# A two-layer decoder trunk on one core: where the last norm sums stand, how weights are scaled, and who computes low parts

## The chip, the cores and the metric

The kernel runs on one core of a Trainium2 chip. Its time is the device time of one execution in microseconds (us), and the figure compared is the median of several executions. The core has a matrix engine (TensorE, PE in the profile; its weight loads are PEld), a vector engine (VectorE, DVE), an activation engine (ScalarE, ACT), GpSimd (POOL) and SyncE (SP), which issues the DMAs. Each engine works through its own list of instructions in order, and waits on semaphores for the others.

## The reference

The reference is a decoder trunk of two layers over 1024 tokens of width 1024, in float32. Cut to what matters here:

```
x   = x + w_out0( concat(conv_module(h), memory_attention(h)) )   # layer 0, h = rms_norm(x)
x   = x + relu(rms_norm(x) @ w_in0)**2 @ w_out_mlp0               # MLP, 1024 -> 4096 -> 1024
kv  = rms_norm(x) @ w_kv                                          # keys and values, made once
x   = x + w_out1( concat(nsa_attention(q, kv), memory_attention(q)) ), q = rms_norm(x) @ w_in
x   = x + relu(rms_norm(x) @ w_in1)**2 @ w_out_mlp1
```

Every rms_norm multiplies a row of x by the inverse root of its mean square and by a gain for each of the 1024 features.

## The kernel before

**Split products.** To keep float32 accuracy with a faster matmul, each operand is held as a high part (`hl[:, 0]`, rounded by ScalarE, L110) and a low part (what the rounding lost, a subtraction, L111). A product is three matmuls: high by high, high by low, low by high (L407 to L409, L448 to L450, L80 to L82). So each weight tile of 128x512 takes a DMA into a buffer `raw`, a ScalarE copy and a subtraction, the last on the engine that `k.lo_eng` names: GpSimd for the weights of the MLPs and output projections, VectorE for those of the attention (`ka`).

**Scaled weights.** The projections into keys, values and queries (`proj`, tile `ps_tok`) take weights that carry the gain of each input feature. `weight` is then called with `scales`, one column of gains for each stretch of 256 (or 292) columns of the tile. For each, ScalarE writes the rounded, scaled high part (L116) and VectorE the scaled low part (L117).

**Halves and stages.** The 1024 tokens are two halves (hf0, hf1) of 512 columns. The program runs: layer 0; the output projection `w_out` and MLP of layer 0 for hf0; `w_out` of layer 0 and the MLP for hf1, with the projections and attention of hf0 (`attend(0)`) woven between; `w_out` of layer 1 and the last MLP for hf0, with `attend(1)` woven between; then, with nothing left to weave, `w_out` of layer 1 and the last MLP for hf1, to the end. A small queue in the program (`k.pe`, `k.run`) and the framework's scheduler, which works with a model of time, lay the woven work into each engine's list. So an edit of one kind of instruction shifts the order around it on every engine.

**`w_out` and the MLP's norm.** `w_out` takes two output tiles at a time (`ps_wo`, a pair), 48 matmuls; VectorE then adds the residual (L411) and frees the two banks of PSUM, ScalarE squares the result, and `sq_add` adds the squares into `acc` (L141). While attentions are woven in, two banks serve all of `ps_wo`, `ps_i` and `ps_mo`; in the last stage there are four. After its four pairs the rows are scaled for the next matmul (`act`, L416 on ScalarE, L417 on VectorE). `inv_rms` sums `acc` over the partitions by matmuls against ones (`ps_n`, L151), takes the inverse root on VectorE (`rsqrt`, three steps on tiles of four columns, L93 to L97), spreads it by a diagonal (L157) and a matmul (L165), and copies it to `r`. The MLP applies `r` to its first products, so that matmuls `ps_i` may begin before `r` exists: in the last stage `mlp` with `both` takes two tiles of `ps_i` (48 matmuls) and asks for the two steps of `inv_rms` between.

**After the MLP** each tile of x gets its sum (`ps_mo`, L470). **After an attention** its result goes through DRAM (`mixd`, L1077) and comes back as `mix` (L387), is split into `act` (L87, L88), and the next `w_out` can start.

## Time and profile before

| | |
|---|---|
| median of 3 runs | 2445.08 us (2444.04 to 2449.28) |
| the profiled execution, its own time | 2451.38 us |
| its span in the trace | 2449.6 us |
| mean granted TensorE clock | 0.988 |
| TensorE busy | 2362.6 us, 96% of the span, 12098 matmuls |
| VectorE busy | 1669.2 us, 68% |
| ScalarE busy | 1293.3 us, 53% |
| GpSimd busy | 1229.9 us, 50% |

The first lines give the time that is compared and the execution from which all rows below come; it is one execution, 0.26% above the median. The busy times say how much of the span each engine worked. The clock is the mean of what was granted to TensorE, 1.0 being 2.4 GHz; in single stretches it is half that.

### The profile page before, as it was taken

How to read it: one execution, taken by the hardware profiler on the slowest of the kernel's cores; microseconds unless marked ns; L12 is line 12 of the kernel's file. 1: busy time of each engine (PE TensorE's matmuls, PEld its weight loads, DVE VectorE, ACT ScalarE, POOL GpSimd, SP SyncE). 2: the span in 40 equal slices, each digit the busy share in tenths (PEclk: the TensorE clock that was granted, in tenths of full speed). 3: DMA queues.
4: the chain of work that ended last, by engine and by line, in shares of the span. 5: the costliest groups of instructions: out<-in, count | busy, mean ns of one | idle time of the engine just before them, and what ended most of it. 6: DMA issues, size and time to landing. Idle time of an engine off the chain costs nothing.

```text
span 2449.6 us, 36781 instructions
## 1 busy us (share of the span) xinstructions
PE 2362.6 (96%) x12098; PEld 1994.6 (81%) x12098; DVE 1669.2 (68%) x3590; ACT 1293.3 (53%) x2938; POOL 1229.9 (50%) x1060
## 2 busy tenths in 40 slices
PE   5998899999988999999999999999999999999999
PEld 4887687888777988888887888888888887788887
DVE  7897586998668667777436866778787765333333
ACT  5575555333545457777434545666766654333332
POOL 2876544545643256566445324565566542344443
PEclk9999999999999999999999999999999999999999
DMA  5212433323344332322335443322222226233233
GB/s 186 80 55 84 151 97 101 102 92 95 123 128 141 112 115 84 91 79 79 114 103 171 136 130 92 112 64 67 80 80 63 62 67 206 69 95 97 93 96 103
DMA packets 157214, 250.87 MB, mean 102 GB/s; under 512 B 17632, under 2 KB 48992, under 8 KB 156512
## 3 DMA queue, kind: packets, MB, share of 16 engines
q1 hardware_dynamic: 157024, 248.52, 33.0%
q8 instruction: 96, 1.57, 0.3%
q14 instruction: 94, 0.77, 0.1%
HBM read 217.52 MB, written 20.45 MB: 97 GB/s over the span
## 4 chain that ended last, share of the span: by engine, by line
PE 62%; DVE 4%; DMA 3%; issue 2%; ACT 1%; POOL 1%; SPq 0%; ACTq 0%; DVEq 0%; POOLq 0%
PE ps_i L448 7%; PE ps_i L450 7%; PE ps_i L449 7%; PE ps_mo L80 6%; PE ps_mo L82 6%; PE ps_mo L81 6%; PE ps_t L1054 4%; PE ps_s L1010 4%; PE ps_o L1070 2%; PE ps_o L1073 2%; PE ps_tok L688 1%; PE ps_tok L687 1%; PE ps_tok L689 1%; PE ps_wo L409 1%; PE ps_wo L407 1%
## 5 line engine op out<-in xcount | busy, mean ns | idle before, releaser
L111 POOL TENSOR_TENSOR hl<-raw,hl 128x512 fp32r<-128x512 f32 x596 | 778.6, 1317 | 873.8 <-ACT hl L110 830.7
L110 ACT ACTIVATE hl<-raw 128x512 fp32r<-128x512 f32 x648 | 405.1, 630 | 631.6 <-PE ps_i L450 258.1
L470 DVE TENSOR_TENSOR x<-x,ps_mo 128x512 f32<-128x512 f32 x512 | 348.3, 683 | 136.8 <-PE ps_mo L82 133.4
L80 PE MATMUL ps_mo<-hid,hl 128*128 128x512 f32 x1024 | 409.3, 400 | 6.9 <-DVE x L470 6.7
L448 PE MATMUL ps_i<-act,hl 128*128 128x512 f32 x1024 | 407.5, 398 | 8.2 <-DVE x L411 6.9
L450 PE MATMUL ps_i<-act,hl 128*128 128x512 f32 x1024 | 405.7, 396 | 0.0
L449 PE MATMUL ps_i<-act,hl 128*128 128x512 f32 x1024 | 404.0, 395 | 1.2 <-DVE act L417 1.2
L82 PE MATMUL ps_mo<-hid,hl 128*128 128x512 f32 x1024 | 401.2, 392 | 0.0
L81 PE MATMUL ps_mo<-hid,hl 128*128 128x512 f32 x1024 | 400.9, 391 | 0.0
L448 PEld LDWEIGHTS ps_i<-act,hl 128*128 128x128 f32 x1024 | 193.7, 189 | 49.4 <-DVE x L411 7.3
L80 PEld LDWEIGHTS ps_mo<-hid,hl 128*128 128x128 f32 x1024 | 192.3, 188 | 49.5 <-DVE x L470 12.7
L456 DVE SCALAR_TENSOR_TENSOR a<-ps_i,r 128x512 f32<-128x512 f32 x128 | 88.0, 689 | 206.5 <-PE ps_i L450 201.6
L449 PEld LDWEIGHTS ps_i<-act,hl 128*128 128x128 f32 x1024 | 193.6, 189 | 41.8 <-DVE act L417 2.2
L450 PEld LDWEIGHTS ps_i<-act,hl 128*128 128x128 f32 x1024 | 193.5, 189 | 41.9 <-issue 0.5
L82 PEld LDWEIGHTS ps_mo<-hid,hl 128*128 128x128 f32 x1024 | 192.2, 188 | 41.1
L81 PEld LDWEIGHTS ps_mo<-hid,hl 128*128 128x128 f32 x1024 | 192.7, 188 | 37.0 <-issue 0.5
L1021 ACT ACTIVATE prob<-ps_s,small 128x512 f32<-128x512 f32 (+3 forms) x240 | 141.1, 590 | 83.0 <-DVE small L1019 52.7
L1040 POOL TENSOR_TENSOR prob<-prob,small 128x1024 f32<-128x1024 f32 (+3 forms) x120 | 180.0, 1524 | 1.3 <-DVE small L1034 0.8
L1062 DVE TENSOR_TENSOR PT<-ps_t,PT 128x512 fp32r<-128x512 f32 (+1 forms) x220 | 147.0, 671 | 48.2 <-ACT PT L1058 46.9
L1058 ACT ACTIVATE PT<-ps_t 128x512 fp32r<-128x512 f32 (+1 forms) x256 | 142.3, 566 | 60.9 <-PE ps_t L1054 55.0
L1010 PE MATMUL ps_s<-KS,Q 128*128 128x512 f32 (+5 forms) x552 | 143.1, 358 | 0.0
L88 DVE TENSOR_TENSOR hid<-a,hid 128x512 fp32r<-128x512 f32 x128 | 100.6, 787 | 59.0 <-ACT hid L87 58.3
(295 smaller groups left out, 4708.8 us busy)
## 6 DMA issues: line engine op xcount, KB each, us to landing
raw<-in_w_mlp_in_dram SPq DMA_DIRECT2D x256, 256.0 KB, 2.8
raw<-in_w_mlp_out_dram SPq DMA_DIRECT2D x256, 256.0 KB, 2.9
raw<-in_w_out_dram SPq DMA_DIRECT2D x64, 256.0 KB, 3.3
Q<-Q SPq DMA_DIRECT2D x160, 64.0 KB, 2.0
raw<-in_cmp_w_dram SPq DMA_DIRECT2D x32, 256.0 KB, 2.7
raw<-in_a_w_dram SPq DMA_DIRECT2D x24, 256.0 KB, 3.0
raw<-in_b_wq_dram SPq DMA_DIRECT2D x24, 256.0 KB, 2.7
mixd<-ev SPq DMA_DIRECT2D x80, 64.0 KB, 2.1
```

Source lines behind the costliest of these rows:

```text
L80: nc.tensor.matmul(ps, lhsT=lh, rhs=rh, start=(i == 0), stop=False)
L81: nc.tensor.matmul(ps, lhsT=lh, rhs=rl, start=False, stop=False)
L82: nc.tensor.matmul(ps, lhsT=ll, rhs=rh, start=False, stop=(i == n - 1))
L110: nc.scalar.activation(hl[:, 0, :n], raw[:, :n], AF.Copy)
L111: k.last_lo = k.lo_eng.tensor_tensor(hl[:, 1, :n], raw[:, :n], hl[:, 0, :n].bitcast(F32), op=ALU.subtract)
L448: nc.tensor.matmul(p_, lhsT=wh, rhs=h[kt][:, 0], start=kt == 0, stop=False)
L449: nc.tensor.matmul(p_, lhsT=wh, rhs=h[kt][:, 1], start=False, stop=False)
L450: nc.tensor.matmul(p_, lhsT=wl, rhs=h[kt][:, 0], start=False, stop=kt == KT - 1)
L470: nc.vector.tensor_add(x[o], x[o], ps)
L1010: nc.tensor.matmul(o_, lhsT=lhs, rhs=rhs, start=(n_ == 0), stop=(n_ == len(mms) - 1))
L1040: nc.gpsimd.tensor_tensor(t, t, sc[:, :, None].to_broadcast([P, 2, t.shape[-1]]), op=ALU.mult)
L1062: nc.vector.tensor_sub(PT[:, 1, :m], Tv[:, :m], PT[:, 0, :m].bitcast(F32))
```

## The change

In `weight` with scales, ScalarE first scales `raw` in place (a new line, 117 in the changed file), then one ScalarE copy over the whole tile makes the high part (118), and one subtraction over the whole tile the low part (120), in turn on GpSimd and VectorE. In `rsqrt` the order of the factors changes, so that with `m` and `t` in PSUM no instruction takes two operands from there; `col_stats` puts `m`, `t` and the last result into free columns of `ps_n`. `k.lo_eng` is VectorE for the `w_out` and the first part of the MLP that follow the projections of `attend(0)` and `attend(1)`, and GpSimd again from the second chunk of the MLP (`c == 1`); `sq_add` follows it. The squares behind the first MLP's second half go to VectorE as well, and three low parts in `conv_norm` move to it. Last, `w_out` of hf1 in layer 1 is no longer run to its end (by `list`) ahead of the MLP: its `inv_rms` is now asked for from within the MLP, and its pool `wb` stays open. (In the code, attention's projections are emitted ahead of `out0(1)` and of `w_out` of layer 1, and woven with them.)

Over the whole program, by the lists of instructions: 112 ScalarE instructions L116 and 112 VectorE instructions L117 go; 112 ScalarE scalings, 64 ScalarE copies and 64 low parts (32 on GpSimd, 32 on VectorE) come. 56 low parts L111 and 29 sums L141 move from GpSimd to VectorE, and 3 of L88. The matmuls are the same in number.

```diff
--- before.py
+++ after.py
@@ -46,7 +46,7 @@
         self.now = 0.0
         self.queue = []
         self.seq = 0
-        self.running = False
+        self.running = self.turn = False
 
     def pe(self, ns):
         self.now += ns
@@ -88,13 +88,14 @@
             (eng or nc.vector).tensor_tensor(lo, src, hi.bitcast(F32), op=ALU.subtract))
 
 
-def rsqrt(nc, r, m, t):
+def rsqrt(nc, r, m, t, last=None):
+
 
     nc.vector.tensor_scalar(r.bitcast(I32), m.bitcast(I32), -0.5, 1597463007.0, op0=ALU.mult, op1=ALU.add)
-    for _ in range(3):
-        nc.vector.tensor_mul(t, r, r)
-        nc.vector.scalar_tensor_tensor(t, t, -0.5, m, op0=ALU.mult, op1=ALU.mult)
-        nc.vector.scalar_tensor_tensor(r, t, 1.5, r, op0=ALU.add, op1=ALU.mult)
+    for i in range(3):
+        nc.vector.tensor_mul(t, r, m)
+        nc.vector.scalar_tensor_tensor(t, t, -0.5, r, op0=ALU.mult, op1=ALU.mult)
+        nc.vector.scalar_tensor_tensor(r if last is None or i < 2 else last, t, 1.5, r, op0=ALU.add, op1=ALU.mult)
 
 
 def weight(k, src, scales=None, pool=None, raw=None):
@@ -113,9 +114,10 @@
         w = n // len(scales)
         for i, g in enumerate(scales):
             s = slice(i * w, (i + 1) * w)
-            nc.scalar.activation(hl[:, 0, s], raw[:, s], AF.Copy, scale=g)
-            nc.vector.scalar_tensor_tensor(hl[:, 1, s], raw[:, s], g, hl[:, 0, s].bitcast(F32),
-                                           op0=ALU.mult, op1=ALU.subtract)
+            nc.scalar.activation(raw[:, s], raw[:, s], AF.Copy, scale=g)
+        nc.scalar.activation(hl[:, 0, :n], raw[:, :n], AF.Copy)
+        k.turn = not k.turn
+        (nc.gpsimd if k.turn else nc.vector).tensor_tensor(hl[:, 1, :n], raw[:, :n], hl[:, 0, :n].bitcast(F32), op=ALU.subtract)
     return hl[:, :, :n]
 
 
@@ -150,11 +152,13 @@
         for j in range(4):
             nc.tensor.matmul(ps[:, j:j + 1], lhsT=a[:, j * P:(j + 1) * P], rhs=k.ones[:, 0:1],
                              start=(i == 0 and j == 0), stop=(i == len(parts) - 1 and j == 3))
-    m, r, t = (k.tmp.tile([P, 4], F32, tag=n_, name=n_, bufs=2) for n_ in ("nm", "nr", "nt"))
+
+    r = k.tmp.tile([P, 4], F32, tag="nr", name="nr", bufs=2)
+    m, t, last = (ps[:, 4 * i:4 * i + 4] for i in range(1, 4))
     nc.vector.tensor_scalar(m, ps[:, 0:4], 1.0 / n, eps, op0=ALU.mult, op1=ALU.add)
-    rsqrt(nc, r, m, t)
+    rsqrt(nc, r, m, t, last)
     d = k.tmp.tile([P, 4, P], F32, tag="diag", name="diag", bufs=1)
-    nc.vector.tensor_mul(d, k.ident[:, None, :].to_broadcast([P, 4, P]), r[:, :, None].to_broadcast([P, 4, P]))
+    nc.vector.tensor_mul(d, k.ident[:, None, :].to_broadcast([P, 4, P]), last[:, :, None].to_broadcast([P, 4, P]))
     return d
 
 
@@ -409,7 +413,7 @@
                     nc.tensor.matmul(ps[i], lhsT=wl, rhs=mix[kt][:, 0], start=False, stop=kt == order[-1])
         for i in range(WG):
             nc.vector.tensor_add(x[o + i], ps[i], rs[i])
-            sq_add(k, acc, x[o + i], o + i == 0, nc.vector if o + i > 5 else None)
+            sq_add(k, acc, x[o + i], o + i == 0, nc.vector if o + i > 5 else k.lo_eng)
         k.pe(24 * WG * HF / 2.4)
     for o in range(KT):
         a, g = mix[order[o]], k.cols[:, (C_MLP0, C_MLP1)[l] + o:][:, 0:1]
@@ -474,6 +478,8 @@
 
     cur = proj_in(0)
     for c in range(NC):
+        if c == 1:
+            k.lo_eng = nc.gpsimd
         nxt = proj_in(c + 1) if c + 1 < NC else None
         proj_out(c, cur, c == NC - 1)
         cur = nxt
@@ -662,7 +668,7 @@
         t = k.tmp.tile([P, HF], F32, tag="a", name="t", bufs=2)
         nc.scalar.activation(t, c, AF.Tanh, bias=b)
         nc.vector.scalar_tensor_tensor(t, t, 1.0, z, op0=ALU.add, op1=ALU.mult)
-        a, b = split(nc, mix[i][:, 0], mix[i][:, 1], t, nc.gpsimd if n in LOP else None)
+        a, b = split(nc, mix[i][:, 0], mix[i][:, 1], t, nc.gpsimd if early and n in LOP else None)
         k.marks += [a, b] if n > 3 else []
 
 
@@ -1258,7 +1264,7 @@
                 if o == 0:
                     acc.append(acc_tile(k))
                 nc.sync.dma_start(xs[hf, :, o], x[hf][o])
-                sq_add(k, acc[0], x[hf][o], o == 0)
+                sq_add(k, acc[0], x[hf][o], o == 0, nc.vector)
             return after
 
         ka = K()
@@ -1300,6 +1306,8 @@
                       Vd)
 
         attend(0, acc)
+
+        k.lo_eng = nc.vector
         r = out0(1)
         acc = []
         mlp(k, 0, x[1], act[1], r, after0(1, acc), MIXORD)
@@ -1309,14 +1317,15 @@
         act = [act_tiles(hf) for hf in range(2)]
         x = [x_tiles(hf) for hf in range(2)]
         load_mix(k, act[0], mixd[0], MIXORD, k.wpool, "raw", k.nraw)
+        k.lo_eng = nc.vector
         rs = [w_out(k, 1, act[0], x[0], xs[0], MIXORD)]
         ka.rpool = pool(es, "rb", "right")
 
         ps3 = es.enter_context(psum_pool("ps3"))
-        with tc.tile_pool(name="wb", bufs=1, side="right") as wb:
-            ka.psum, ka.wpool, ka.tmp, ka.tag = ps3, wb, wb, "mm"
-            load_mix(ka, act[1], mixd[1], MIXORD, ka.wpool, "mix", 8)
-            rs.append(iter(list(w_out(ka, 1, act[1], x[1], xs[1], MIXORD))))
+        wb = pool(es, "wb", "right")
+        ka.psum, ka.wpool, ka.tmp, ka.tag = ps3, wb, wb, "mm"
+        load_mix(ka, act[1], mixd[1], MIXORD, ka.wpool, "mix", 8)
+        rs.append(w_out(ka, 1, act[1], x[1], xs[1], MIXORD))
         for hf in range(2):
             if hf == 1:
                 k.psum, k.nps = ps3, 4
```

Lines of the changed file stand 1 to 9 further down than before (L111 is L112, L117 became 117 to 120, L141 is L143, L151 is L153, L411 is L415, L417 is L421, L448 is L452, L470 is L474).

**VectorE at the start of the projections of `attend(0)`**, around the first sums of `ps_wo` for hf1 in layer 0. Before:

```order
L470 TENSOR_TENSOR x_2551<-x_2551,ps_mo 128x512 x2
L664 SCALAR_TENSOR_TENSOR t<-t,z 128x512
L470 TENSOR_TENSOR x_2552<-x_2552,ps_mo 128x512 x2
L88 TENSOR_TENSOR act_347<-t,act_347 128x512
L664 SCALAR_TENSOR_TENSOR t<-t,z 128x512
L117 SCALAR_TENSOR_TENSOR hl<-raw,cols,hl 128x256 x8
L411 TENSOR_TENSOR x_5968<-ps_wo,rs 128x512 x2
```

and in the changed kernel:

```order
L88 TENSOR_TENSOR act_345<-t,act_345 128x512
L143 TENSOR_TENSOR acc<-acc,sq 128x512
L88 TENSOR_TENSOR act_346<-t,act_346 128x512
L143 TENSOR_TENSOR acc<-acc,sq 128x512 x2
L120 TENSOR_TENSOR hl<-raw,hl 128x512
L112 TENSOR_TENSOR hl<-raw,hl 128x512 x2
L120 TENSOR_TENSOR hl<-raw,hl 128x512
L415 TENSOR_TENSOR x_5960<-ps_wo,rs 128x512
L158 TENSOR_SCALAR ps_n<-ps_n 128x4
L112 TENSOR_TENSOR hl<-raw,hl 128x512
L94 TENSOR_SCALAR nr<-ps_n 128x4
L415 TENSOR_TENSOR x_5960<-ps_wo,rs 128x512
```

Eight scaled low parts L117 in a row stood ahead of the two L411; now two L120, two low parts of other weights (L112) and, above them, sums of squares that were GpSimd's (L143) stand there, and the second L415 comes four instructions behind the first.

**TensorE where the `w_out` of the last stage ends and the last MLP begins** (`ps_n` are the norm sums, `ps_i` the MLP's first products). Before:

```order
L408 MATMUL ps_wo<-act_18493,hl 128x512
L409 MATMUL ps_wo<-act_18493,hl 128x512
L151 MATMUL ps_n<-ones,acc 128x1 x4
L448 MATMUL ps_i<-act_18494,hl 128x512
L449 MATMUL ps_i<-act_18494,hl 128x512
```

and in the changed kernel, 32 matmuls after the last `ps_wo`:

```order
L454 MATMUL ps_i<-act_18490,hl 128x512
L452 MATMUL ps_i<-act_18491,hl 128x512
L453 MATMUL ps_i<-act_18491,hl 128x512
L153 MATMUL ps_n<-ones,acc 128x1 x4
L454 MATMUL ps_i<-act_18491,hl 128x512
L452 MATMUL ps_i<-act_18491,hl 128x512
```

The sums stood directly behind the last `ps_wo`; now 32 of the 48 matmuls of the first two tiles of `ps_i` stand between.

**VectorE at the end of `attend(1)`**, where `mix` comes back (`ev` is the last piece of the attention, `x` the sums of the MLP that is woven in). Before:

```order
L1076 TENSOR_TENSOR ev<-ps_o,ev 64x256
L470 TENSOR_TENSOR x_18501<-x_18501,ps_mo 128x512
L470 TENSOR_TENSOR x_18498<-x_18498,ps_mo 128x512 x2
L88 TENSOR_TENSOR act_18494<-mix,act_18494 128x512
L470 TENSOR_TENSOR x_18499<-x_18499,ps_mo 128x512
L88 TENSOR_TENSOR act_18495<-mix,act_18495 128x512
L88 TENSOR_TENSOR act_18496<-mix,act_18496 128x512
L470 TENSOR_TENSOR x_18499<-x_18499,ps_mo 128x512
```

and in the changed kernel:

```order
L1082 TENSOR_TENSOR ev<-ps_o,ev 64x256
L474 TENSOR_TENSOR x_18500<-x_18500,ps_mo 128x512
L474 TENSOR_TENSOR x_18501<-x_18501,ps_mo 128x512 x2
L88 TENSOR_TENSOR act_18494<-mix,act_18494 128x512
L88 TENSOR_TENSOR act_18495<-mix,act_18495 128x512
L88 TENSOR_TENSOR act_18496<-mix,act_18496 128x512
```

Sums of the MLP stood between the splits of `mix`; now the last sums all come before them. On TensorE the last matmul of `attend(1)` (`ps_o`, from `Vc`) was followed by 54 matmuls `ps_mo` before the first `ps_wo`; in the changed kernel 18 follow it.

## Rows read from the trace of the kernel before

**Rows 1.** The page's first part: busy us, share of the span, instructions.

```profile
PE 2362.6 (96%) x12098; PEld 1994.6 (81%) x12098; DVE 1669.2 (68%) x3590; ACT 1293.3 (53%) x2938; POOL 1229.9 (50%) x1060
```

**Rows 2.** Windows: stretch, its length, each engine's busy us (count), granted clock, DMA.

```profile
650.00:800.00 150.00, 132.76 (x675) 110.97 (x674) 119.44 (x237) 81.64 (x162) 64.16 (x47) 0.95 0.47 143
...
1290.00:1500.00 210.00, 198.29 (x1156) 170.44 (x1155) 146.71 (x324) 102.09 (x208) 80.46 (x63) 0.99 0.45 137
...
2000.00:2110.00 110.00, 102.95 (x466) 83.10 (x465) 55.64 (x90) 45.84 (x77) 26.71 (x21) 0.97 0.42 137
```

**Rows 3.** Windows of 7 us behind four waits of TensorE.

```profile
691.00:698.00 7.00, 6.06 (x16) 4.80 (x17) 1.48 (x3) 2.07 (x4) 2.52 (x3) 0.56 0.66 214
777.00:784.00 7.00, 6.26 (x18) 5.00 (x19) 6.04 (x27) 3.01 (x5) 0.31 (x1) 0.61 0.13 44
2041.00:2048.00 7.00, 7.00 (x32) 5.63 (x31) 2.38 (x4) 1.98 (x4) 2.85 (x3) 1.00 1.02 377
2090.00:2097.00 7.00, 7.00 (x22) 5.85 (x23) 2.97 (x13) 0.00 (x0) 0.00 (x0) 0.53 0.00 0
```

**Rows 4.** Timeline at 685 to 692: start, us, engine, line, instruction, [idle before, releaser].

```profile
684.74 0.40 PE L409 MATMUL ps_wo<-act,hl 128*128 128x512 f32 x1
691.94 0.79 PE L407 MATMUL ps_wo<-act,hl 128*128 128x512 f32 x1 [6.80 <-DVE x L411]
...
681.06 10.23 DVE L117 SCALAR_TENSOR_TENSOR hl<-raw,cols,hl 128x256 fp32r<-128x256 f32 x8 [3.86 <-ACT hl L116]
```

**Rows 5.** Timeline at 745 to 778, of TensorE, VectorE and GpSimd.

```profile
770.45 0.40 PE L409 MATMUL ps_wo<-act,hl 128*128 128x512 f32 x1
777.74 0.80 PE L448 MATMUL ps_i<-act,hl 128*128 128x512 f32 x1 [6.90 <-DVE x L411]
...
745.30 0.68 DVE L411 TENSOR_TENSOR x<-ps_wo,rs 128x512 f32<-128x512 f32 x1
...
772.10 1.26 DVE L93 TENSOR_SCALAR hr<-hm 128x8 int32<-128x8 int32 x1
...
777.02 0.67 DVE L411 TENSOR_TENSOR x<-ps_wo,rs 128x512 f32<-128x512 f32 x1
...
773.62 3.33 POOL L111 TENSOR_TENSOR hl<-raw,hl 128x512 fp32r<-128x512 f32 x2 [0.28 <-ACT hl L110]
```

**Rows 6.** Waits of TensorE, 1290 to 1500: waited for, us in total, times, longest.

```profile
PE ps_c L820 <- DVE hT L797: 1.4, 1, 1.4
```

**Rows 7.** Timeline at 2086 to 2090, of TensorE and VectorE.

```profile
2086.62 0.40 PE L409 MATMUL ps_wo<-act,hl 128*128 128x512 f32 x1
2089.89 1.87 PE L151 MATMUL ps_n<-ones,acc 128*128 128x1 f32 x8 [2.87 <-DVE acc L141]
...
2089.15 0.68 DVE L141 TENSOR_TENSOR acc<-acc,sq 128x512 f32<-128x512 f32 x1
```

**Rows 8.** Timeline at 2024 to 2042, of TensorE, VectorE and SyncE's queue.

```profile
2024.03 0.28 PE L1070 MATMUL ps_o<-PT,Vc 128*128 128x256 f32 x1
...
2041.34 0.39 PE L407 MATMUL ps_wo<-act,hl 128*128 128x512 f32 x1
...
2040.30 0.67 DVE L470 TENSOR_TENSOR x<-x,ps_mo 128x512 f32<-128x512 f32 x1
...
2027.35 3.65 SPq L387 DMA_DIRECT2D mix<-mixd  x8
...
2033.72 1.69 SPq L107 DMA_DIRECT2D raw<-in_w_out_dram  x3
```

**Rows 9.** Lines by form: count, duration min/median/max in ns, first and last start.

```profile
L117 DVE SCALAR_TENSOR_TENSOR hl<-raw,cols,hl x112: 465/484/1541, 681.1 to 1472.0; 128x256 fp32r<-128x256 f32 x96, 128x292 fp32r<-128x292 f32 x16
L116 ACT ACTIVATE hl<-raw,cols x112: 491/500/542, 680.5 to 1471.5; 128x256 fp32r<-128x256 f32 x96, 128x292 fp32r<-128x292 f32 x16
L111 POOL TENSOR_TENSOR hl<-raw,hl x596: 1267/1296/1987, 42.4 to 2435.1; 128x512 fp32r<-128x512 f32 x199
L111 DVE TENSOR_TENSOR hl<-raw,hl x52: 674/689/1810, 36.4 to 2077.1; 128x512 fp32r<-128x512 f32 x52
```

## Prediction

> **What bounds the kernel now.** I read the page's first part before anything else: TensorE is busy for 96% of the span, VectorE for 68%, the others less [rows 1]. As the change neither adds nor removes matmuls, it can only win what TensorE spends idle or at half clock, and lose by making more of it. Next I cut the span into windows and looked for stretches where TensorE's busy time falls short. From 650 us on there are three: 17.2 us idle of 150 where the attention of the first half begins, 11.7 of 210 where that of the second begins, 7.1 of 110 around the end of that attention and the start of the last MLP [rows 2]. That is 36 us of the 87 that TensorE idles in the whole span [rows 1]; the other 51 lie at the start, in layer 0 and at the very end, where the change moves little. In these windows the granted clock is also below 1. Windows of 7 us behind the long waits show 0.56, 0.61 and 0.53 [rows 3], which is the lower level, 1.2 GHz, for most of each. Such a window costs 7 us times what is missing from 1: 3.1, 2.7 and 3.3 us.
>
> Last I read the timeline at each wait, for what comes last there.
>
> - Wait A, at 685 us: TensorE issues the last matmul of a pair at 684.74 and starts the next at 691.94, released by VectorE's L411, which frees the banks [rows 4]. A matmul at full clock is followed by the next after 0.23 us (some 31 in 7 us [rows 3]), so 7.0 us are lost. L411 was ready, but eight L117 stood ahead of it and took 10.23 us, 1.28 us each, where the median of an L117 is 0.484 us [rows 4, 9].
> - Wait B, at 770 us: 7.1 us, again for L411 [rows 5]. Here steps on tiny tiles, such as L93 on 128x8, take 1.26 us while GpSimd runs low parts of 1.3 to 1.9 us; L411 starts only at 777.02.
> - Wait C, 1290 to 1500 us: the 11.7 us are many small waits, the largest 1.4 us [rows 6].
> - Wait D, at 2087 us: the norm sums `ps_n` wait 2.87 us for the last sum L141, which ends at 2089.83; then comes the stretch at 0.53 [rows 3, 7].
> - Place E, at 2024 to 2041 us: from the last matmul of the attention to the first `ps_wo` 17.3 us pass, in which 54 matmuls `ps_mo` keep TensorE going; 54 by 0.23 is 12.4 us, so it idles for 4.9 [rows 8].
>
> **The change, part by part.** VectorE loses 112 L117, by the median 54 us [rows 9]. It gains 56 low parts, 29 sums and three splits of GpSimd's, and 32 scaled low parts, some narrower, so about 120 steps: at 0.69 us or less [rows 9] some 79 us. Net that is up to +25 us of VectorE, half of it near each attention, less what its steps no longer lose to a busy GpSimd. GpSimd loses 88 steps of 1.3 us, takes 32 back, and so gets some 70 us. ScalarE gains 64 steps, about 40 us, and at 53% [rows 1] has room for them.
>
> *A.* In the new order four subtractions of about 0.69 us, 2.8 us, stand where eight L117 took 10.2. But the second scaled low part belongs to a later weight: its buffer must come free first (there are three), through a GpSimd step of 1.3 us and a transfer. If all of that falls into the wait, 5 us remain; if none, nothing. I take 2.5 us, halfway, and since the 2.9 us of wait D were enough to be followed by the low clock, I leave that loss in place. Saved: 7.0 - 2.5 = 4.5 us, with ends 0 and 10.1.
>
> *B.* From the last L411 of the third pair (745.30) to the first of the fourth (777.02) VectorE went 31 us [rows 5], over eight L117, six L417 and steps stretched by GpSimd. The new list has two scaled low parts in place of the eight, as many L417, and four low parts and two sums more; at unstretched durations I count about 24 us (an estimate). TensorE ran for 24.5 us from 745.98 to its stop at 770.7 (770.45 [rows 5]). The wait should nearly go, and the low clock with it: of 7.1 + 2.7 = 9.8 us I take 9, with ends 3 and 10.
>
> *C.* VectorE is busy for 147 of 210 us there [rows 2]; its net gain of up to 12 us fits in, but small waits of this sort follow the order, which is new everywhere. I take +2, with ends -5 and +6.
>
> *D.* In the new order 32 matmuls, 7.3 us, stand between the last `ps_wo` and the sums, while the last L141 ends 3.0 us behind that `ps_wo` [rows 7]. So the wait is gone. The inverse root starts later but is covered by 34 more matmuls, 7.8 us. Saved: 2.9 + 3.3 = 6.2 us; if the clock falls for another reason, 2.9.
>
> *E.* Now only 18 matmuls `ps_mo`, 4.1 us, follow the attention's last one; the other 36 have moved ahead of it, where TensorE was full already. What the 17.3 us consist of does not change: result to DRAM and back (`mix` is issued at 2027.35), splits, the weights of `w_out` (issued at 2033.72, into buffers that the splits free) [rows 8]. The sums L470 that stood between the splits and ahead of the first low part (one at 2040.30) are out of the way; for these I take 1.5 us off. So 17.3 - 1.5 - 4.1 = 11.7 us idle in place of 4.9, 6.8 more. Before, the broken wait left the clock at 1.00 [rows 3]; behind one whole wait of that length I expect the lower level as behind A, B and D, 3.3 us. Together -10 us, with ends -4 and -12.
>
> *The rest.* `rsqrt` on PSUM columns has as many steps as before, off TensorE's path in the last stage; they cost nothing as long as those 34 matmuls cover them, else some tenths of a microsecond each time. The path of a scaled weight grows by a ScalarE copy and, every second time, by GpSimd's 1.3 us. TensorE takes 24 matmuls of half of 0.23 us, 2.8 us, for each; ScalarE needs 1.6 and GpSimd 0.65 on average, so the rate holds and only first weights come later. I take -2 us, with ends 0 and -15 (below).
>
> Sum: 4.5 + 9 + 2 + 6.2 - 10 - 2 = 9.7 us. The profiled execution took 2451.4 us, its span 2449.6, so 2441.7 by the sum; it lies 6.3 us above the median of the runs, and from the median 2445.1 the sum gives 2435.
>
> **A rule on the port.** L117 takes 0.484 us in the median and 1.28 where GpSimd works without a pause [rows 4, 9], and a step of 8 columns takes 1.26 beside GpSimd [rows 5]: a VectorE step with two inputs in SBUF can last until GpSimd's instruction ends. The Trainium skill, "SBUF — State Buffer", section "SBUF: two separate sides", says the same: the two engines share a port pair that is locked for a whole instruction, and a VectorE operation with two SBUF inputs is fully blocked by a GpSimd one that reads SBUF. The trace agrees, with 1541 ns as the longest L117. The rule speaks for moving steps off GpSimd, and against the 32 new low parts that it gets amid the projections, where L117 ran at 0.484.
>
> **Rivals.**
>
> *VectorE becomes the late engine (slower).* Each of the 32 GpSimd low parts may hold up a VectorE step by up to 1.3 - 0.48 = 0.8 us, 26 us in all, on top of the net 25. Around 650 to 800 us VectorE was busy for 119 of 150 us [rows 2]; with its half of the two it would need 145, and TensorE would wait for it at each L411 and each scaled weight. Then A and B save nothing, C goes to -5, the rest to -15 and D and E stay: -5 + 6.2 - 10 - 15 = -24, 2469 us; with half of that 2457. It decides from the point where A, B and C together save less than the 5.8 us by which E and the rest exceed D. Against it: GpSimd loses far more steps than it gets, the 1.28 us of A came from its unbroken work, and the short steps gain too.
>
> *The banks are freed no earlier (same).* If A's L411 still stands behind the transfer of a scaled weight and B keeps 4 us and its clock, A and B together save 3: 3 + 2 + 6.2 - 10 - 2 = -1, 2446 us. For it: the release of L411 depends on the list around it, and not on L117 alone.
>
> *E is cheaper (faster still).* If the clock stays up at E and the return of `mix` is as quick as its transfers allow, E is -4 and B 10: about 2428; with all of A 2422.
>
> That the change does not do what it says is excluded for D by the new order; for E the order shows the 18 matmuls.
>
> **How the numbers follow.** The forecast as summed, 5 to 15 us faster, gets 0.48; the faster rival 0.16; same 0.18; slower 0.18. A change within 0.2%, 4.9 us, can't be told from none here. The faster side thus has 0.64. The range leaves out one in ten at each end: 2420, where all of the faster rival comes in, to 2453, short of the half-priced slower rival.
>
> **What would show it.** Behind `ps_wo` in the last stage no wait for L141, and a clock of 1.0 at the first `ps_i`. At the end of the second attention one wait of TensorE of about 12 us for the first weights of `w_out`, and a low clock behind it. At the first L411 of the projections a wait of about 2.5 us, at the last hardly one. VectorE's busy total between 1670 and 1700, GpSimd's about 1160. I am wrong if waits for scaled low parts or for L411 in the projections add up to over 10 us in either attention, or if other work fills place E.

## The result, and the profile after

The changed kernel takes 2463.64 us, the median of six runs (2461.86 to 2465.38), and the kernel before 2448.53 us; the ratio is 1.0063, with a 95% interval of 1.0049 to 1.0076. The forecast was 10 us faster; it is 15 us slower, and outside the range. None of the rivals describes it: places D and E went as written, place B did not, and the largest part came from something that no step of the prediction had looked at.

The page of the changed kernel's profiled execution (span 2461.6 us, clock 0.984), its first part:

```profile
PE 2372.0 (96%) x12098; PEld 1994.3 (81%) x12098; DVE 1649.2 (67%) x3598; ACT 1326.1 (54%) x3002; POOL 1143.4 (46%) x1004
```

TensorE has the same 12098 matmuls as in [rows 1], but is busy for 9.4 us more. More waiting can't do that: either its clock was lower or its matmuls themselves became longer. That is the first thing to explain, and stretches at full clock tell the two apart (below). VectorE is busy for 20 us less and GpSimd for 86 us less, where the prediction had up to 30 us more for VectorE. Fewer steps stretched beside GpSimd would do that (v48 below shows it for L117), but the 20 us were not taken apart.

The same windows as in [rows 2], and two narrower ones around waits A and B (stretch, its length, busy us of TensorE, weight loads, VectorE, ScalarE, GpSimd, granted clock, DMA):

```profile
650.00:800.00 150.00, 136.43 (x693) 114.51 (x692) 115.16 (x257) 91.11 (x183) 21.72 (x19) 0.94 0.46 144
670.00:700.00 30.00, 27.17 (x116) 21.68 (x115) 23.58 (x47) 22.31 (x43) 2.66 (x2) 0.94 0.65 210
755.00:795.00 40.00, 29.26 (x162) 24.76 (x162) 34.04 (x97) 20.83 (x46) 6.21 (x5) 0.83 0.34 110
1290.00:1500.00 210.00, 200.24 (x1161) 172.44 (x1160) 141.55 (x324) 115.09 (x231) 39.45 (x36) 0.98 0.42 130
1500.00:2000.00 500.00, 497.82 (x2821) 430.97 (x2820) 384.19 (x1030) 340.01 (x936) 296.83 (x264) 1.00 0.26 79
2000.00:2110.00 110.00, 96.76 (x457) 79.86 (x456) 55.93 (x85) 44.34 (x75) 22.17 (x19) 0.94 0.39 127
```

and in the kernel before the two narrow ones, and the one from 1500 us on:

```profile
670.00:700.00 30.00, 21.73 (x84) 17.05 (x83) 17.83 (x17) 14.81 (x29) 24.53 (x18) 0.89 0.56 180
755.00:795.00 40.00, 31.45 (x175) 25.82 (x174) 35.05 (x95) 19.84 (x44) 10.76 (x9) 0.91 0.37 112
1500.00:2000.00 500.00, 500.00 (x2850) 435.04 (x2849) 386.15 (x1028) 338.50 (x938) 299.57 (x266) 1.00 0.26 76
```

Around A (670 to 700) TensorE's idle time falls from 8.3 to 2.8 us and the clock rises from 0.89 to 0.94: about 7 us won. Around B (755 to 795) idle time rises from 8.6 to 10.7 us and the clock falls from 0.91 to 0.83: about 5 us lost. Around C idle time falls from 11.7 to 9.8, which 0.01 of clock over 210 us gives back, and 2.2 us are new behind it. The last window has 13.2 us idle in place of 7.1.

What waits there, in the timeline of the changed kernel (TensorE, GpSimd and VectorE, 678 to 787 us):

```profile
678.58 0.77 PE L411 MATMUL ps_wo<-act,hl 128*128 128x512 f32 x1 [2.83 <-DVE x L474]
...
754.68 1.69 POOL L724 TENSOR_TENSOR mq<-mq,qg 128x512 f32<-128x512 f32 x1 [6.39 <-DVE mq L723]
...
755.12 1.80 DVE L421 SCALAR_TENSOR_TENSOR act<-x,cols,act 128x512 fp32r<-128x512 f32 x1
...
773.52 0.68 DVE L415 TENSOR_TENSOR x<-ps_wo,rs 128x512 f32<-128x512 f32 x1
...
774.25 0.80 PE L452 MATMUL ps_i<-act,hl 128*128 128x512 f32 x1 [4.75 <-DVE x L415]
...
782.17 0.69 DVE L112 TENSOR_TENSOR hl<-raw,hl 128x512 fp32r<-128x512 f32 x1 [1.70 <-ACT hl L111]
...
782.77 0.15 DVE L97 SCALAR_TENSOR_TENSOR ht<-ht,hr 64x1 f32<-64x1 f32 x1
...
785.96 0.22 DVE L88 TENSOR_TENSOR khl<-kcn,khl 64x64 fp32r<-64x64 f32 x1
...
786.23 0.37 PE L833 MATMUL ps_dc<-ident,khl 64*128 64x64 f32 x1 [3.98 <-DVE khl L88]
```

At A one wait of 2.83 us is left. At B L415 comes at 773.52 and TensorE has waited 4.75 us for it; in [rows 5] it was 6.90. But VectorE now waits 1.70 us for a ScalarE copy, and behind the low part L112 that needs it stand the remaining small steps of an inverse root of the attention (`ht`, L97), laid in turn with those of another root and of the norm. The tile `khl`, which comes out of that root, is made only at 785.96, and TensorE waits another 3.98 us for it. The L421 of 1.80 us runs beside GpSimd's L724: a stretched step, as in [rows 5].

The timeline from behind the second attention to the last norm sums (TensorE, ScalarE, SyncE's queue):

```profile
2041.27 0.39 PE L82 MATMUL ps_mo<-hid,hl 128*128 128x512 f32 x1
2054.90 0.79 PE L411 MATMUL ps_wo<-act,hl 128*128 128x512 f32 x1 [13.24 <-ACT hl L111]
...
2054.22 1.92 ACT L111 ACTIVATE hl<-raw 128x512 fp32r<-128x512 f32 x3 [1.40 <-DMA raw<-in_w_out_dram]
...
2047.90 2.61 SPq L108 DMA_DIRECT2D raw<-in_w_out_dram  x3
...
2109.87 0.95 PE L153 MATMUL ps_n<-ones,acc 128*128 128x1 f32 x8
```

and three windows (columns as above):

```profile
784.00:791.00 7.00, 4.77 (x19) 4.15 (x20) 5.78 (x21) 3.01 (x8) 1.46 (x2) 0.51 0.17 61
...
2055.00:2061.00 6.00, 6.00 (x15) 4.66 (x16) 1.86 (x3) 1.73 (x3) 0.00 (x0) 0.53 0.70 252
2109.00:2116.00 7.00, 7.00 (x36) 5.82 (x35) 2.52 (x12) 1.26 (x2) 3.03 (x3) 1.00 0.26 77
```

After its last `ps_mo` TensorE waits 13.24 us for the weights of `w_out`, whose transfers are issued at 2047.90, and its clock is at 0.53 for the 6 us behind. That is place E, answering to [rows 8]. The norm sums at 2109.87 have no wait, and the 7 us from 2109 on run at 1.00 where [rows 3] had 0.53: place D.

Now the longer matmuls. Two stretches of 48 each from the dense last stage, first and last start of `ps_i` and of `ps_mo`, in the changed kernel:

```profile
2203.78 0.39 PE L452 MATMUL ps_i<-act,hl 128*128 128x512 f32 x1
...
2214.75 0.39 PE L454 MATMUL ps_i<-act,hl 128*128 128x512 f32 x1
2214.98 0.39 PE L80 MATMUL ps_mo<-hid,hl 128*128 128x512 f32 x1
...
2225.65 0.39 PE L82 MATMUL ps_mo<-hid,hl 128*128 128x512 f32 x1
```

and in the kernel before:

```profile
2215.47 0.40 PE L448 MATMUL ps_i<-act,hl 128*128 128x512 f32 x1
...
2226.25 0.39 PE L450 MATMUL ps_i<-act,hl 128*128 128x512 f32 x1
2226.47 0.40 PE L80 MATMUL ps_mo<-hid,hl 128*128 128x512 f32 x1
...
2237.18 0.39 PE L82 MATMUL ps_mo<-hid,hl 128*128 128x512 f32 x1
```

From the first start to the last are 47 steps. `ps_mo` takes 10.67 us in the changed kernel, 10.71 before: 227 and 228 ns a matmul. `ps_i` takes 10.97 against 10.78 us: 233.4 and 229.4 ns, at a granted clock of 1.00 and with no wait in either. `ps_i` streams `act`, `ps_mo` streams `hid`. The list of tiles of the two built programs says where these stand in SBUF (the byte in each partition, and its remainder by 512):

```
tile          before          after
hl (weights)   4928  320       4928  320
hid           31552  320      31552  320
act, first    62592  128      62464    0
```

The change took two tiles, `nm` and `nt`, twice 32 bytes each, out of the pool `tmp`. `act` stands behind that pool, and so moved by 128 bytes, as did the tiles behind `act`, those of x among them.

### The profile page after: what moved, and what is told of

Its sections match the earlier page's. It is cut to its first block, busy times and chain, and to the rows that moved or that the text cites. A ratio compares the mean times of both kernels' runs of the same rounds, so it can differ in the third digit from the quotient of the medians.

```text
span 2461.6 us, 36812 instructions
## 1 busy us (share of the span) xinstructions
PE 2372.0 (96%) x12098; PEld 1994.3 (81%) x12098; DVE 1649.2 (67%) x3598; ACT 1326.1 (54%) x3002; POOL 1143.4 (46%) x1004
## 4 chain that ended last, share of the span: by engine, by line
PE 85%; DVE 6%; DMA 3%; issue 3%; ACT 2%; POOL 1%; SPq 0%; POOLq 0%; ACTq 0%; DVEq 0%
PE ps_i L452 9%; PE ps_i L453 9%; PE ps_i L454 9%; PE ps_mo L80 9%; PE ps_mo L82 8%; PE ps_mo L81 8%; PE ps_t L1060 4%; PE ps_s L1016 4%; PE ps_o L1076 2%; PE ps_wo L411 2%; PE ps_o L1079 2%; PE ps_wo L412 2%; PE ps_wo L413 2%; PE ps_a L80 2%; PE ps_a L82 2%
## 5 line engine op out<-in xcount | busy, mean ns | idle before, releaser
L112 POOL TENSOR_TENSOR hl<-raw,hl 128x512 fp32r<-128x512 f32 x540 | 696.2, 1300 | 759.0 <-ACT hl L111 736.4
L111 ACT ACTIVATE hl<-raw 128x512 fp32r<-128x512 f32 x648 | 405.4, 630 | 630.1 <-PE ps_i L454 251.6
L474 DVE TENSOR_TENSOR x<-x,ps_mo 128x512 f32<-128x512 f32 x512 | 348.8, 684 | 139.1 <-PE ps_mo L82 136.2
L452 PE MATMUL ps_i<-act,hl 128*128 128x512 f32 x1024 | 408.6, 399 | 7.4 <-DVE x L415 7.2
L452 PEld LDWEIGHTS ps_i<-act,hl 128*128 128x128 f32 x1024 | 192.8, 188 | 51.9 <-DVE x L415 7.4
L120 POOL TENSOR_TENSOR hl<-raw,hl 128x512 fp32r<-128x512 f32 (+1 forms) x32 | 38.5, 1205 | 219.2 <-ACT hl L118 185.5
```

The lines of the kernel that those rows point to most:

```text
L111: nc.scalar.activation(hl[:, 0, :n], raw[:, :n], AF.Copy)
L112: k.last_lo = k.lo_eng.tensor_tensor(hl[:, 1, :n], raw[:, :n], hl[:, 0, :n].bitcast(F32), op=ALU.subtract)
L452: nc.tensor.matmul(p_, lhsT=wh, rhs=h[kt][:, 0], start=kt == 0, stop=False)
L474: nc.vector.tensor_add(x[o], x[o], ps)
```

## The experiments

Theory 1 is that the time of a matmul depends on the place of the operand that it streams against the place of its weights. Theory 2 is that `ps_i` became slower by the new order of instructions or by chance of the execution. Theories D and E are the prediction's steps of that name. Each run has its own comparison with the kernel before; its median was 2447.2 to 2447.8 us in these runs.

| run | median us | ratio to before (95%) | matmuls, 2150 to 2400 us |
|---|---|---|---|
| before | 2447 | 1 | 1096 |
| the change | 2463.6 | 1.0063 (1.0049 to 1.0076) | 1088 |
| a128 | 2451.45 | 1.0018 (1.0008 to 1.0027) | 1096 |
| a320 | 2445.16 | 0.9990 (0.9981 to 1.0000) | 1104 |
| b384 | 2460.92 | 1.0056 (1.0040 to 1.0072) | 1088 |
| b192 | 2442.43 | 0.9978 (0.9968 to 0.9989) | 1104 |
| hid192 | 2454.29 | 1.0029 (1.0012 to 1.0045) | 1088 |
| all192 | 2449.16 | 1.0013 (1.0002 to 1.0023) | 1095 |
| mq320 | 2430.26 | 0.9938 (0.9920 to 0.9955) | |
| z192 | 2437.25 | 0.9960 (0.9949 to 0.9972) | |
| w48 | 2437.39 | 0.9952 (0.9937 to 0.9968) | |
| v48 | 2432.44 | 0.9933 (0.9916 to 0.9949) | |
| r80 | 2442.01 | 0.9973 (0.9964 to 0.9982) | |
| best | 2432.39 | 0.9935 (0.9920 to 0.9950) | |
| wz48 | 2429.56 | 0.9938 (0.9917 to 0.9959) | |
| wzl48 | 2431.27 | 0.9942 (0.9922 to 0.9962) | |
| wv48 | 2445.54 | 0.9993 (0.9982 to 1.0003) | |

The last column counts matmuls in a window of 250 us in the last stage, in which TensorE is busy throughout.

### The place of act

**a128, a320 (the changed kernel), b384, b192 (the kernel before).** A pool with one unused tile stands ahead of `act`; nothing else changes.

```diff
         k.rpool = k.tmp
+        pool(es, "gap").tile([P, 32], F32, name="gap")
         ap = pool(es, "act")
```

with 32 columns (128 bytes), 80, 96 and 48. The order on each engine is that of the kernel it was made from.

> The changed kernel with 128 bytes of unused room ahead of the pool of act, so that act stands at the byte it had before the change; every engine's order is that of the changed kernel. Theory 1 (the place of act in SBUF sets TensorE's pace: 229.7 ns per 512-column ps_i matmul before, 233.3 after, on some 4500 matmuls that read act): pace back to about 229.7 ns and a time of 2446 to 2450 us. Theory 2 (the pace comes from the new order of instructions, or from the execution): pace stays at 233.3 ns, time 2463.6 us.

> The changed kernel with 320 bytes ahead of the pool of act, which then stands at the same remainder by 512 bytes (320) as the weights hl and as hid, whose matmuls took 227 ns in both kernels. Theory 1: ps_i falls to about 227 ns, and the time to 2433 to 2438 us. Theory 1b (only the place of act itself counts, not against that of the weights): somewhere between 227 and 233 ns. Theory 2: 233.3 ns, 2463.6 us.

> The kernel before with 384 bytes ahead of the pool of act, so that act stands at remainder 0 by 512 as in the changed kernel, and nothing else changed. Theory 1: ps_i at 233.3 ns, some 14 to 18 us slower than before, 2462 to 2466 us. Theory 2: 229.7 ns, 2448.5 us.

> The kernel before with 192 bytes ahead of the pool of act, so that act stands at remainder 320 by 512, as hl and hid do. Theory 1: ps_i at 227 ns, 10 to 12 us faster than before, 2436 to 2439 us. Theory 2: no change, 2448.5 us.

By the pace of the matmuls theory 1 holds in all four, theory 2 in none. The times lie 1.1 us (b384) to 7.2 us (a320) outside what was expected, each on the side of a smaller effect. With `act` at remainder 0 the kernel before becomes 13.5 us slower, and the changed kernel with `act` at its old byte 12.2 us faster. At 320, where the weights and `hid` stand, both are faster than at 128. In a320 a `ps_i` takes as long as a `ps_mo` (timeline, first and last of 48):

```profile
2211.26 0.39 PE L452 MATMUL ps_i<-act,hl 128*128 128x512 f32 x1
...
2221.91 0.39 PE L454 MATMUL ps_i<-act,hl 128*128 128x512 f32 x1
```

10.65 us by 47 is 226.6 ns. The gains at 320 (5.0 us in b192, 6.3 in a320 against a128) are smaller than the 10 to 12 expected. `ps_i` alone, 2.8 ns by 3072, would give 8.6 us. The traces show what is missing: the 2.8 ns belong to the last stage. Taken over the whole program, from the start of one `ps_i` to the start of the next (full clock, steps under 260 ns), the mean is 229.5 ns before and 227.9 in b192; 1.6 ns by 3072 are 4.9 us. From 1500 to 2000 us, beside the attention, it is 230.3 and 230.4 ns, so the better place wins nothing there, while the change's place still costs: 233.5.

**hid192, all192.** The same gap in the kernel before, between the weights and `hid`, and ahead of the weights:

```diff
         k.wpool = pool(es, "w")
+        pool(es, "gap").tile([P, 48], F32, name="gap")
         k.hid = pool(es, "hid")
```

> The kernel before with 192 bytes between the pool of the weights and that of hid, so that hid stands at remainder 0 by 512, act at 320 and the weights hl at 320 as ever. Theory 1 (place of the streamed operand against the weights, for every tile alike): ps_mo from 227 to about 233 ns, ps_i at 227 ns, time about 15 us above that with act at 320, 2457 to 2462 us. Rival (something in act's pool alone): ps_mo stays at 227 ns, 2442 us.

> The kernel before with 192 bytes ahead of the weights, so that hl and hid stand at remainder 0 by 512 and act at 320: every distance between them as before, every place moved. Theory 1b (only the distance of streamed operand and weights counts): ps_mo 227 ns, ps_i 229.7 ns, time as before, 2445 to 2450 us. Rival 1a (the place of the streamed operand counts, 0 slow and 320 fast): ps_mo about 233 ns, ps_i 227 ns, 2457 to 2462 us.

The time of hid192 is 2.7 us under what was expected, that of all192 within it. In hid192 the two change roles (timeline, first and last start of 48 `ps_mo`, then of 48 `ps_i`):

```profile
2206.05 0.39 PE L80 MATMUL ps_mo<-hid,hl 128*128 128x512 f32 x1
...
2217.02 0.39 PE L82 MATMUL ps_mo<-hid,hl 128*128 128x512 f32 x1
2217.25 0.39 PE L448 MATMUL ps_i<-act,hl 128*128 128x512 f32 x1
...
2227.92 0.39 PE L450 MATMUL ps_i<-act,hl 128*128 128x512 f32 x1
```

`ps_mo` takes 10.97 us by 47, 233.4 ns, and `ps_i` 10.67, 227.0. So it is not a property of `act`. In all192 the weights, `hid` and `act` have all moved, but not against each other, and the count of matmuls (1095) is that of before; the time is 2 us above, at the edge of its interval. So the distance counts, not the place. With streamed operand and weights at the same remainder a matmul of 512 columns takes 227 ns; at a distance of 320 (streamed less weights) 229.4; at 192, which is the change's, 233.4. Within a block the weights stand at four columns of a tile, 512 bytes apart. In the changed kernel and in a320 the times of `ps_i` do not differ between these by 0.1 ns (in the kernel before the first column's are 1.4 ns longer), so I read the distance by 512.

The traces hold more distances. The `w_out` of the last stage takes its weights from another pool, `wb`, whose tiles `hl` stand at remainder 288 in the kernel before, 416 in the changed one and 320 in best (below). Its 192 matmuls `ps_wo` of 512 columns, from start to start as above:

| run | act | weights in wb | distance by 512 | ns |
|---|---|---|---|---|
| best | 320 | 320 | 0 | 226.8 |
| b192 | 320 | 288 | 32 | 233.3 |
| the change | 0 | 416 | 96 | 233.3 |
| a128 | 128 | 416 | 224 | 233.3 |
| before | 128 | 288 | 352 | 233.3 |
| a320, mq320 | 320 | 416 | 416 | 234.2, 234.3 |

So 32 bytes of distance already cost as much as any other, and 320 with its 229.4 ns is the exception.

### The end of the second attention, and the last norm sums

**mq320.** The changed kernel at 320, with the first MLP's squares left on GpSimd; by the order, 54 matmuls then follow the second attention's last one.

```diff
-                sq_add(k, acc[0], x[hf][o], o == 0, nc.vector)
+                sq_add(k, acc[0], x[hf][o], o == 0)
```

> The changed kernel except that the squares behind the first MLP stay on GpSimd, and with act at remainder 320 by 512 bytes, as in the run with 320 bytes. By the order, 54 matmuls again follow the last one of the second attention, not 18. Theory E (the missing 36 matmuls cost 8 to 9 us of waiting and 3 to 7 us of low clock): 10 to 15 us under the run with 320 bytes (2445.2), so 2430 to 2435 us. Rival (they only moved the wait, and the loss turns up elsewhere): 2443 to 2447 us.

Against a320 14.9 us are won. TensorE's waits from 2000 to 2110 us (waited for, us in total, times, longest):

```profile
PE ps_mo L80 <- DVE x L474: 2.1, 2, 1.4
PE ps_wo L411 <- ACT hl L111: 0.4, 1, 0.4
```

The wait, 13.1 us in a320, is gone, as theory E had it. But not all of the 14.9 us is E: from 1290 to 1500 us the clock is 1.00 in mq320 and 0.98 in a320, which is 4 us, and from 650 to 800 us mq320 idles 2 us more at a clock lower by 0.01. wzl48 below also shows that the price of the place alone is smaller than this pair says.

**z192.** The kernel before at 320, with the last part of the change alone (the difference for `rs.append` and `wb`, as shown in the change).

> The kernel before with the last part of the change alone (the last norm sums taken from within the MLP, pool wb left open), and act at remainder 320 by 512. Against the kernel before with act at 320 (2442.4): theory D (the 2.9 us wait and the stretch at the low clock both go): 2436 us, and no stretch at the low clock behind 2080 us. Rival (the clock falls at the change of stage anyway): 2439 to 2440 us.

5.2 us against b192, by theory D 6.4; the intervals of the two just touch. The window in which the sums stand (2088.01 us) runs at the full clock, and no wait is left in it:

```profile
2083.00:2090.00 7.00, 7.00 (x36) 5.94 (x35) 2.23 (x9) 1.68 (x3) 2.52 (x2) 1.00 0.11 38
```

### Scaling, VectorE's steps, and both

**w48, v48, r80.** The kernel before at 320 with one part each: the scaling of weights; VectorE's low parts and sums (`k.lo_eng`, and `conv_norm`); `rsqrt`. The edits are those parts of the change, with a gap that puts `act` at 320.

> The kernel before with the scaling of weights alone changed (ScalarE in place, one low part in turn on GpSimd and VectorE), act at remainder 320; compare with 2442.4 us. Theory (the run of eight L117 was what kept L411 waiting at 685 and 770 us): both waits of 7 us fall under 3 us, 2430 to 2436 us. Rival (the low parts that GpSimd gets amid the projections hold VectorE up, or the longer path of a weight does): at least one of the waits stays above 4 us, 2440 us or more.

> The kernel before with the move of low parts, of the squares in w_out and of three low parts in conv_norm from GpSimd to VectorE alone, act at remainder 320; compare with 2442.4 us. Theory (VectorE's steps are no longer stretched beside GpSimd, so the waits for L411 shrink although it has more to do): 2434 to 2439 us, the L117 at 681 to 691 us near 0.5 us each. Rival (VectorE becomes the late engine): 2444 us or more.

> The kernel before with the new order of factors in rsqrt and its columns in PSUM alone; act at remainder 320 by 512 bytes, with the gap made larger by what the removed tiles took. Theory 1 and the step of the prediction (no cost by itself, all of its effect on the time came through the place of act): 2440 to 2445 us. Rival (steps on PSUM are dearer and lie on the path): over 2447 us.

Against 2442.4 us, w48 wins 5.0, v48 10.0 and r80 nothing. r80 shows that the steps of `rsqrt` on PSUM cost nothing that these runs can see, and that what this part did to the time it did through the tiles that it removed. In w48 the waits for L411 (its line 412) are down to 0.8 us; the longest wait of TensorE from 650 to 800 us is a new one, for GpSimd's scaled low part (its line 119 is the 120 of the change):

```profile
PE ps_tok L689 <- POOL hl L119: 2.7, 1, 2.7
```

Its time is 1.4 us above what I expected. In v48 six L117 take 3.27 us in one go, where [rows 4] had eight in 10.23:

```profile
680.02 3.27 DVE L117 SCALAR_TENSOR_TENSOR hl<-raw,cols,hl 128x256 fp32r<-128x256 f32 x6 [0.23 <-ACT hl L116]
```

So they had been stretched by GpSimd, and with its steps moved away they are not. The gain is more than I had expected (2434 to 2439), and its trace does not show where all of it comes from. The two waits for L411, 6.7 and 6.9 us in b192, shrink to one of 3.2, but two others are new (TensorE, 650 to 800 us):

```profile
PE ps_n L165 <- DVE diag L157: 4.6, 1, 4.6
PE ps_wo L407 <- ACT sq L140: 4.3, 1, 4.3
PE ps_i L448 <- DVE x L411: 3.2, 1, 3.2
```

Idle time there falls from 17.4 us to 12.3, and the clock from 0.95 to 0.93, which takes 3 us of that back.

**best.** mq320 with two more gaps, on the right side of SBUF, that bring the weights of the projections and of the last `w_out` to remainder 320.

```diff
+            tc.tile_pool(name=f"gw{hf}", bufs=1, side="right") as gw, \
             tc.tile_pool(name=f"wa{hf}", bufs=1, side="right") as k.wpool:
+        gw.tile([P, 40], F32, name="gap2")
...
+        pool(es, "gap3", "right").tile([P, 24], F32, name="gap3")
         wb = pool(es, "wb", "right")
```

> As the run without the moved squares (2430.3 us, act at 320), and besides the weights of the attentions and of the last stage's w_out moved to remainder 320 too, by gaps of 160 and 96 bytes. Theory 1: the 192 matmuls of the last w_out fall from 234 to 227 ns, 1.3 us, and if the 256-column matmuls of the projections follow the same rule, 2 to 4 us more: 2425 to 2429 us. Rival (narrow matmuls don't): 2429 us.

No gain: 2432.4 against 2430.3, with intervals that overlap. The traces show both parts. The last `w_out` did as expected, 226.8 ns in place of 234.3, 1.4 us for its 192 matmuls. The projections' matmuls of 256 columns (`ps_tok`) did not follow: they take 119.7 ns from start to start at the same remainder and 118.3 in mq320. So here the rule is seen at 512 columns alone.

**wz48, wzl48, wv48.** The kernel before at 320 with scaling and norm sums; with these and VectorE's steps in the second half; with scaling and VectorE's steps in both halves (the line below ahead of `out0(1)` too, and `conv_norm`).

```diff
+        k.lo_eng = nc.vector
         rs = [w_out(k, 1, act[0], x[0], xs[0], MIXORD)]
```

> The kernel before with the scaling of weights and the last norm sums changed, nothing moved to VectorE, act at remainder 320. Theory (these two are independent and the extra steps of VectorE are what brings waits back at 760 to 780 us): 2437.4 - 5 = 2431 to 2433 us, with no wait over 3.5 us between 650 and 800 us. Rival (waits come with any new order): 2436 us or more.

> As the run before (scaling and norm sums), with VectorE's low parts and sums in the second half alone added; by the order, 18 matmuls instead of 54 then follow the second attention's last one. Theory E: 10 to 15 us above the run before, with one wait of 12 to 14 us near 2030 us and a long stretch at the low clock behind it. Rival (what that end costs is won back between 1290 and 1500 us): within 4 us of it.

> The kernel before with the scaling of weights and all of VectorE's extra steps but the squares behind the first MLP, act at remainder 320. By the order it too has 18 matmuls at the end of the second attention. Theory (the combination makes VectorE late again): between 650 and 800 us two waits of over 3 us and two stretches at the low clock, where scaling alone had none over 3; with the dear end of the attention, 2446 to 2452 us. Rival (the two parts add up): no wait over 3 us between 650 and 800 us, 2436 to 2442 us.

wv48 loses what w48 and v48 had won: 2445.5 us, 0.5 us under the range of the theory. One part of it is place E. By the order wv48 has 18 matmuls behind the second attention's last one, where w48 and v48 have 54 (v48 has the same VectorE steps: the number follows the whole order, not one part). In its trace the first `ps_wo` behind them waits 13.5 us. From 2000 to 2110 us its TensorE idles 16.3 us at a clock of 0.92, that of w48 and v48 6.3 and 7.0 us at 0.98. The other part is the first attention. The window from 650 to 800 us in w48, v48 and wv48:

```profile
650.00:800.00 150.00, 141.49 (x747) 120.11 (x746) 111.92 (x222) 97.56 (x197) 85.10 (x61) 0.99 0.47 148
...
650.00:800.00 150.00, 137.72 (x720) 117.25 (x719) 121.37 (x277) 83.75 (x168) 19.42 (x14) 0.93 0.46 146
...
650.00:800.00 150.00, 135.60 (x710) 115.01 (x710) 118.20 (x252) 91.94 (x189) 30.69 (x24) 0.94 0.45 144
```

With scaling alone TensorE idles 8.5 us there at a clock of 0.99; with VectorE's steps alone 12.3 at 0.93; with both, 14.4 us at 0.94. And the waits of TensorE in wv48, same stretch:

```profile
PE ps_n L166 <- DVE diag L158: 4.5, 1, 4.5
PE ps_wo L408 <- ACT sq L141: 4.4, 1, 4.4
PE ps_i L449 <- DVE x L412: 4.1, 1, 4.1
```

These are the three waits of v48; mq320 has them too (4.4, 4.4, 4.1). So VectorE's steps bring them, with scaling or without, and what scaling wins at the first attention is lost with them. In the changed kernel the order differs again: of its three waits (2.8, 4.7 and 4.0 us) only that for L415 is of the same kind. That such waits come from where the steps stand in VectorE's list was read from the timeline of the changed kernel above, and not tried by itself.

wz48 has the lowest median of all, with none of the other low parts and sums moved to VectorE; mq320, 0.7 us above, cannot be told from it. It is 1.4 us under its expected range, and its longest wait from 650 to 800 us is 2.8 us. Two of its windows:

```profile
1290.00:1500.00 210.00, 197.85 (x1162) 172.07 (x1161) 133.67 (x286) 114.42 (x240) 100.10 (x79) 0.98 0.40 128
2000.00:2110.00 110.00, 107.55 (x480) 86.11 (x479) 56.97 (x92) 45.53 (x75) 33.14 (x25) 1.00 0.41 141
```

and those of wzl48:

```profile
1290.00:1500.00 210.00, 199.69 (x1174) 174.28 (x1173) 141.32 (x322) 114.67 (x241) 52.34 (x46) 0.98 0.40 128
2000.00:2110.00 110.00, 96.61 (x431) 78.82 (x430) 53.70 (x90) 43.85 (x73) 18.77 (x15) 0.94 0.39 133
```

From 1290 to 1500 us wzl48 has 1.8 us less idle time, and in the last window 10.9 us more at a clock of 0.94. By the medians it is only 1.7 us slower, by the spans of the two profiles 7.5 (2434.0 and 2426.5), with runs of each from 2428 to 2437. So the expectation of 10 to 15 us failed, and its rival holds in part: some of what that end costs is won ahead of it. How much of E is net stays open between 2 and 8 us.

## Why the prediction was wrong, point by point

- **What bounds the kernel** was right for waits, and wrong in one sentence: that without more matmuls the change "can only win what TensorE spends idle or at half clock, and lose by making more of it". The time of a matmul itself can change. The changed kernel lost 12.2 us so (a128 against the change).
- **The rest** (-2) was the step that failed most. It took `rsqrt` and its PSUM columns for free, and so they are as steps (r80), but the tiles that went with them moved `act` by 128 bytes. Over the whole program the 3072 matmuls `ps_i` took 233.3 ns in place of 229.6 in a128, 11.5 us, and the 768 `ps_wo`, which stream `act` as well, 233.3 in place of 230.4, 2.2 us; by the medians the place cost 12.2 us.
- **A** (+4.5) was about +7, by the windows; the wait left was 2.8 us. That this is near the estimated 2.5 is luck: it is a wait for another step, a sum L474, and at the L415 that the estimate was about no wait is left.
- **B** (+9) failed: it was about -5. The count of VectorE's work assumed unstretched steps one behind the other with nothing awaited. The wait for L415 did shrink, to 4.75 us, but VectorE then waited for ScalarE with the small steps of inverse roots behind it, TensorE idled 4 us more, and the clock fell twice. Scaling alone (w48) does remove this wait; v48 and wv48 show that VectorE's extra steps bring waits of 3 to 5 us with them.
- **C** (+2) was nothing, with 2.2 us of new idle time behind it, from 1500 to 2000 us.
- **D** (+6.2) was right: no wait and full clock in the changed kernel, 5.2 us in z192.
- **E** (-10) was right in place and kind: 13.2 us of waiting in place of 4.9, forecast 11.7, and the low clock behind it, 6 us at 0.53, 2.8 us. Its net price is smaller (wzl48).
- **The sum** of these waits and clocks is 7 - 5 + 0 - 2 + 6 - 11 = -5 us, where +9.7 was forecast. a128, with the old place, is 4.1 us slower than before, which agrees. With the 12.2 us of the place, that makes the 16 us between the change and 2447.4.
- **The rival of a late VectorE** has its mechanism in part (v48, wv48), but not its price, and not by the route described: VectorE's busy time fell. The rule that it leaned on held up: in the Trainium skill's page "SBUF — State Buffer", section "SBUF: two separate sides", a VectorE step with two SBUF inputs is blocked by a GpSimd step that reads SBUF and began first. The trace agrees (L421 takes 1.80 us, begun 0.44 us into GpSimd's L724 of 1.69 us), and as L117's in v48 show, it worked for the move of steps off GpSimd. One row that the prediction put under this rule does not belong there: L93, 1.26 us in [rows 5], has one input. The trace of the kernel before shows that it too ended with a step of GpSimd (L111, 771.48 to 773.34; L93 to 773.36).

## What to carry to other kernels

Before pricing an edit, compare the places of the tiles that the busiest engine reads in the two built programs: an edit that removes 128 bytes can cost more than all that it saves in waits. Where TensorE is the bound and streams 512 columns against weights, put the streamed tile and the weights at the same remainder by 512 bytes; here that was worth 5 us in the kernel before, and 18 in the changed one. Two parts of a change that help alone (5 and 10 us here) can come to nothing together, because each new order of the lists can open a wait somewhere else; so each is tried alone and in pairs, and the whole timeline is read, not only the place that the edit meant.

## What the runs showed of the hardware

A matmul of 512 columns with float32r operands took 227, 229.4 or 233.4 ns at full granted clock, by the distance of its streamed operand from its weights in SBUF (0, 320 or 192 bytes by 512), with no other change, and 233.3 to 234.3 at each of the other five distances that the traces hold. Beside the attention, from 1500 to 2000 us, distance 0 lost its advantage over 320 (230.4 and 230.3 ns). Why is not shown; weights are loaded while matmuls stream (in the changed kernel loads keep their part busy for 1994 us and matmuls TensorE for 2372, of 2462), but no run here separates the two reads. The Trainium skill's page "SBUF — State Buffer", section "SBUF: two separate sides", says that only the port pair of VectorE and GpSimd causes contention and that TensorE never waits on anyone. As to other engines no run here tests it; that an operand's place is free for TensorE it would be wrong to conclude, by the 2.8% between 227 and 233.4 ns.

The clock behind a long wait: after 13.2 us of idling it stayed at 0.53 for 6 us of work, not longer than the stretches of [rows 3] behind waits of 3 to 7 us.
